# One scheduling priority in an RWKV scan: the merge of every pair's inverted blocks is ranked with the scan's steps

## The chip, the cores and the metric

The kernel runs on one core of a Trainium2 chip, as one launch. The metric is the device time of that launch in microseconds (us), less being better. Several executions are timed and their median is given; one further execution is recorded by the hardware profiler, and all rows shown here come from that one.

## The reference

The program computes two blocks of a network. The first block runs two layers of attention mixers (dilated attention with gated linear attention, then window attention with latent attention), each with a gated feed-forward part. The second block runs a gMLP mixer, a mixture of experts, an RWKV mixer and a second mixture of experts, on 512 tokens of grid data and 256 tokens of context, 1024 channels each. The change concerns the RWKV mixer alone, whose core is a recurrence over the tokens in both directions, for 16 heads of 64 channels:

```python
def _wkv_step(S, inp):
    r_t, w_t, k_t, v_t, a_t, b_t = inp
    sa = jnp.einsum('zbhvk,zbhk->zbhv', S, a_t)
    S = S * w_t[..., None, :] + sa[..., :, None] * b_t[..., None, :] + v_t[..., :, None] * k_t[..., None, :]
    return S, jnp.einsum('zbhvk,zbhk->zbhv', S, r_t)

def wkv_bidir(state0, scan_in):
    state, ys = lax.scan(_wkv_step, state0, scan_in)
    ys = jnp.moveaxis(ys, 0, 2)
    return state, ys[0] + ys[1][:, ::-1]
...
    state_c, y_c = wkv_bidir(state0, scan_c)
    _, y_l = wkv_bidir(state_c, scan_l)
```

The state of a head is a 64x64 matrix. It first goes through the 256 tokens of context, then through the 512 tokens of the grid.

## The kernel before

The class `_RwkvScan` does the recurrence in chunks of 64 tokens. The heads go in eight pairs, p0 to p7, and a pair has 12 scan steps (768 tokens in chunks of 64). One step works on both heads and both directions. Inside a chunk the recurrence is a triangular system, and its 64x64 triangle is inverted beforehand: two 32x32 diagonal blocks by substitution, and the block below them by two products, which is the merge that the change is about.

What a pair needs before its first step is made while the pair ahead of it is being scanned:

- **Elementwise preparation and triangles** (`pre`, L2309 to L2393): decays, keys and so on, on DVE and ACT; the triangles by PE matmuls L2376, masked by DVE L2381 into `AAx` (shown as tile `xT`). It runs two pairs ahead.
- **Substitution** (`load_tri`, `subst`, `back`): four DMAs L2404 take the triangles to DRAM, L2408 brings them back with another layout, GpSimd (POOL) substitutes column after column (L2420 and L2424, 31 times each), L2431 and four L2437 bring the result back through DRAM into `rwXT`, the tile of inverses, of which there are two.
- **Merge** (`merge`): DVE transposes the inverted blocks (L2449), PE multiplies (48 matmuls of 32x32 L2456), ACT evicts (four L2463), PE multiplies again (48 times L2471), and ACT evicts into `rwXT` (four L2479).
- **Operands** (`load_prep`, `prep`): DMA L2285 loads `inv`, PE makes products (L2516, L2522, 64 rows by 128), DVE masks them into `AAk` and `AAr` (L2525, L2527), PE transposes (L2531, L2540), ACT evicts (L2532, L2543), PE adds up within the chunk (L2555), ACT evicts (L2562, L2563). They come in three parts of four steps each; only the first must be there before the pair's first step.
- **Output** (`out`): DMA L2664 loads the gate into `AAk` (a name with two buffers, which the DVE masks use also), L2699 stores the result. From the seventh pair on the output projection (`project_out`) runs too: DMAs L2724, L2749 and L2751, matmuls in three float32 passes (L266 to L268), DVE L2739 and L245, ACT L244.

A scan step is a chain over the engines: DVE makes the right side `rwrz` (L2609, in a pair's first step L2611), PE multiplies it by the inverse `rwXT` (L2616), ACT evicts that as `UV` (L2620, one per step, called U below), PE updates the state (L2625), DVE adds it (L2634, L2636), and PE multiplies the new state for the next step (L2600, L2605).

`run` records the steps of a pair and between them the work of `beside`, in shares that fit the pair's length. The order of instructions on each engine is then decided by a scheduler, which ranks them by priority; inside `tc.high_priority(offset=400)` an instruction is ranked 400 ahead of where it was recorded. All scan steps are recorded so, and of the merges that of pair 7 alone. Every engine, and SP's queue of DMA issues, then runs its list in that order, and an instruction that waits holds all behind it.

Of the kernel before, what the change touches and what calls it, by code (L numbers as in the profile page):

```python
# [193 lines left out]
class Kern:  # L194
# [1718 lines left out]
    def rwkv_project(self, c, R, dr):  # L1913
# [76 lines left out]
        def full(j, w, name, ntok, ahead, beside, extra=None):  # L1990

            view = lambda f: [(0, w[:, f * P : (f + 1) * P])]
            early = [weights(view(f), P) for f in range(ahead)]
            cut = [(t0, min(T, ntok - t0)) for t0 in range(0, ntok, T)]
            outs = [[(self.pp.tile([P, 512], F32, tag="mm", name="mmps"), *c) for c in cut] for _ in early]
            x = []
            for d in range(KD):
                x.append(mix(j, d, ntok))
                for (H, L), out in zip(early, outs):
                    for ps, t0, n in out:  # L2000
                        self.mm3(
                            ps[:, :n], H[:, d, :], L[:, d, :], x[d][0][:, t0 : t0 + n], x[d][1][:, t0 : t0 + n],
                            d == 0, d == KD - 1,
                        )
            W = weights(view(ahead), P)
            for f in range(ahead):
                store(f, name, outs[f], ntok, extra)
            for f in range(ahead, KD):
                out = product(W, P, x, ntok)
                if f + 1 < KD:  # L2010
                    W = weights(view(f + 1), P)
                for _ in range(2 if f < KD - 1 else KD):
                    next(beside, None)
                store(f, name, out, ntok, extra)
# [49 lines left out]
        gate = []  # L2064
        beside = (s for g in (kk(), thin(5, [([(0, io["rw_g1"][:, a:b])], b - a) for a, b in ((0, 128), (128, 160))], T, gates)) for s in g)
        full(0, io["rw_wr"], "r", T, 2, beside)
        parts = []
        for n, sg, raw, wH, wL in gate:
# [38 lines left out]
class _RwkvScan:  # L2107
# [48 lines left out]
    def beside(self, p):  # L2156

        n = p + 1  # L2160
        inv = self.subst(n) if n < 8 else iter(())
        if n == 7:
            self.wo = self.project_out()
        wo = self.wo if n >= 7 else iter(())
        if n + 1 < 8:
            self.load_pre(n + 1)
        pre = self.pre(n + 1) if n + 1 < 8 else iter(())
        part = lambda g: iter(lambda: next(g, 0), 0)

        def operands():  # L2170
            if p >= 0:
                yield from part(self.gen)
                self.marks.add(("prep", p, 1))
            if p > 0:
                yield from self.out(p - 1)
                self.marks.add(("out", p - 1))
            if p >= 0:
                yield from self.gen
                self.marks.add(("prep", p, 2))
            if n < 8:  # L2180
                self.load_prep(n)
                self.gen = self.prep(n)
                yield from part(self.gen)
                while ("scan", p, 0) not in self.marks:
                    yield None
                yield from part(self.gen)
                self.marks.add(("prep", n, 0))

        def triangles():
            yield from pre  # L2190
            for _ in inv:
                if n == 7:
                    yield None
            if n < 8:
                self.back(n)
                self.marks.add(("subst", n))
            if n + 1 < 8:
                self.load_tri(n + 1)

        i, own, ahead = 0, operands(), triangles()  # L2200
        for w in own:
            yield w
            i += 1
            if i % 2 == 0:
                w = next(ahead, None)
                if w is not None:
                    yield w
            if n >= 7 and i % (2 if n == 7 else 1) == 0:
                w = next(wo, None)
                if w is not None:  # L2210
                    yield w
            for _ in range(2):
                next(inv, None)
        for w in ahead:
            if w is not None:
                yield w
        if n < 8:
            mg = self.merge(n)
            while True:
                with self.K.tc.high_priority(offset=400) if n == 7 else ExitStack():  # L2220
                    w = next(mg, None)
                if w is None:
                    break
                yield w
            self.marks.add(("merge", n))
        while ("scan", p, 2) not in self.marks:
            yield next(wo, None)
        if n == 8:
            yield from self.out(7)
            self.marks.add(("out", 7))  # L2230
            yield from wo
# [556 lines left out]
class _Sumsq:  # L2788
# [25 lines left out]
    def part(self):  # L2814
        if self.sums is None:
            self.flush()
            K, m = self.K, 32 * self.g
            self.sums = K.wk.tile([P, 512], F32, tag="sqs", name="sqs", bufs=1)
            K.nc.vector.tensor_copy(self.sums[:m, : self.n], self.ps[:m, : self.n])
        return self.sums[: 32 * self.g]  # L2820
# [110 lines left out]
```

## Time and profile before

| what | value |
|---|---|
| median of three timed executions | 4237.75 us (4226.5 to 4241.26) |
| profiled execution | 4238.35 us |
| its span, first to last instruction | 4236.2 us |
| mean granted TensorE clock over the span | 0.917 |
| the scan's steps, from the first U to the last | 3011.9 to 3621.3 us of the span |

How to read it: PE is TensorE, DVE is VectorE, ACT is ScalarE, POOL is GpSimd, SP issues the DMAs. A busy PE is not a PE at its peak: the granted clock is 1.00 at 2.4 GHz and 0.50 at 1.2 GHz, and a stretch between has part of each. The profiled execution has 2.15 us around its span. Times in the trace count from the start of the span.

### The profile page before, as it was taken

Reading aid. Unit: us, or ns where it says so; the run is one execution under the profiler, and the core shown is the slowest. Engines: PE = TensorE matmul, PEld = TensorE weight load, DVE = VectorE, ACT = ScalarE, POOL = GpSimd, SP = SyncE. Lnnn points to the kernel's source line nnn. Section 1 sums busy time; section 2 is a strip of 40 time slices with the busy share of each in tenths; the row PEclk is TensorE's granted clock in tenths of the full one; section 3 lists DMA queues with packets and bytes.
Section 4 is the critical chain, followed back from the end, with each engine's and each line's share of the span. In section 5 each row is a group of like instructions: output and inputs, shape, how many; then the busy total and the mean of one; then the engine's idle time right before and its main releaser. Section 6 shows DMA issues by size and latency. Waiting matters only on the chain. (4 is left out here: it accounts for less than half of the span.)

```text
span 4236.2 us, 56567 instructions
## 1 busy us (share of the span) xinstructions
PE 3829.5 (90%) x22652; PEld 2587.6 (61%) x22652; DVE 1814.1 (43%) x3656; ACT 1324.4 (31%) x2612; POOL 603.9 (14%) x829
## 2 busy tenths in 40 slices
PE   8989999999999989999788997997788899688886
PEld 6746777665677769887433333775577777433332
DVE  3443334465433534434422224554657655511112
ACT  3333224344322522234111112434446554200001
POOL 0000100000101000001110002001645442210001
PEclk9969999999999999999899998997768769799998
DMA  3212553211352322121699997342111222499997
GB/s 117 72 56 90 180 194 101 63 57 65 105 196 89 105 63 78 53 102 73 238 408 390 397 398 279 91 155 77 44 50 43 49 57 75 188 378 416 415 413 304
DMA packets 324825, 711.87 MB, mean 168 GB/s; under 512 B 79616, under 2 KB 251904, under 8 KB 299728
## 3 DMA queue, kind: packets, MB, share of 16 engines
q1 hardware_dynamic: 308704, 658.43, 42.7%
q0 software_dynamic: 15856, 49.79, 3.4%
q8 instruction: 180, 2.95, 0.3%
q14 instruction: 85, 0.70, 0.1%
HBM read 666.64 MB, written 47.55 MB: 169 GB/s over the span
## 5 line engine op out<-in xcount | busy, mean ns | idle before, releaser
L266 PE MATMUL mmps<-xH,wH 128*128 128x512 f32 (+1 forms) x1384 | 550.4, 399 | 10.7 <-ACT xH L359 8.2
L267 PE MATMUL mmps<-xL,wH 128*128 128x512 f32 (+1 forms) x1384 | 545.7, 394 | 0.0
L268 PE MATMUL mmps<-xH,wL 128*128 128x512 f32 (+1 forms) x1384 | 544.2, 394 | 0.0
L1488 PE MATMUL bgps<-wg,bxT 128*64 128x512 f32 (+2 forms) x1040 | 474.3, 601 | 0.9 <-issue 0.9
L1489 PE MATMUL bgps<-wu,bxT 128*64 128x512 f32 (+1 forms) x896 | 401.5, 602 | 26.3 <-DMA wu<-in_moe_w_up_dram 26.3
L244 ACT ACTIVATE wH<-wraw 128x512 fp32r<-128x512 f32 (+3 forms) x473 | 264.7, 619 | 500.4 <-PE mmps L267 289.8
L245 DVE TENSOR_TENSOR wL<-wraw,wH 128x512 fp32r<-128x512 f32 (+3 forms) x473 | 320.5, 723 | 212.2 <-ACT wH L244 211.7
L266 PEld LDWEIGHTS mmps<-xH,wH 128*128 128x128 f32 (+1 forms) x1384 | 258.8, 187 | 105.5 <-issue 22.1
L267 PEld LDWEIGHTS mmps<-xL,wH 128*128 128x128 f32 (+1 forms) x1384 | 258.8, 187 | 71.2 <-issue 10.8
L268 PEld LDWEIGHTS mmps<-xH,wL 128*128 128x128 f32 (+1 forms) x1384 | 258.5, 187 | 71.4 <-issue 11.8
L1505 PE MATMUL byps<-wd,bhT 128*64 128x512 f32 (+2 forms) x1040 | 292.5, 649 | 1.1 <-ACT bhT L1496 1.1
L1488 PEld LDWEIGHTS bgps<-wg,bxT 128*64 128x64 f32 (+2 forms) x1040 | 140.1, 138 | 213.8 <-issue 202.2
L1490 ACT ACTIVATE bh<-bgps 64x512 f32<-64x512 f32 (+2 forms) x65 | 38.4, 591 | 641.6 <-PE bgps L1489 545.1
L1489 PEld LDWEIGHTS bgps<-wu,bxT 128*64 128x64 f32 (+1 forms) x896 | 112.8, 129 | 121.9 <-issue 74.4
L1491 DVE TENSOR_TENSOR bh<-bgps,bh 64x512 f32<-64x512 f32 (+1 forms) x56 | 38.6, 690 | 341.1 <-ACT bh L1490 341.1
L2420 POOL TENSOR_TENSOR isub<-xT,rwX 96x31 f32<-96x31 f32 (+15 forms) x248 | 144.0, 581 | 262.9 <-DMA xT<-rwd 244.1
L1505 PEld LDWEIGHTS byps<-wd,bhT 128*64 128x64 f32 (+2 forms) x1040 | 86.5, 145 | 154.5 <-issue 148.8
L2424 POOL TENSOR_TENSOR rwX<-rwX,isub 96x31 f32<-96x31 f32 (+15 forms) x248 | 154.0, 621 | 19.4
L1454 POOL DMA_INDIRECT xg<-hnat,ix x65 | 62.7, 965 | 648.3 <-PE bxps L1476 609.6
L266 PE MATMUL mmps<-mH,pH 128*128 128x512 f32 (+2 forms) x336 | 123.5, 371 | 12.0 <-ACT pH L244 9.1
L532 POOL TENSOR_TENSOR ffng<-ffng,rstd 128x512 f32<-128x512 f32 x44 | 58.9, 1339 | 472.5 <-ACT ffng L531 472.5
L267 PE MATMUL mmps<-mL,pH 128*128 128x512 f32 (+1 forms) x336 | 124.2, 370 | 0.0
(741 smaller groups left out, 7441.4 us busy)
## 6 DMA issues: line engine op xcount, KB each, us to landing
wg<-in_moe_w_gate_dram SPq DMA_DIRECT2D x64, 2048.0 KB, 23.1
wu<-in_moe_w_up_dram SPq DMA_DIRECT2D x61, 2048.0 KB, 21.1
wd<-in_moe_w_down_dram SPq DMA_DIRECT2D x61, 2048.0 KB, 19.7
adaw<-in_ada_w_dram SPq DMA_DIRECT2D x48, 1024.0 KB, 5.0
wraw<-in_ffn_w_gate_dram SPq DMA_DIRECT2D x22, 1024.0 KB, 5.4
wraw<-in_ffn_w_up_dram SPq DMA_DIRECT2D x22, 1024.0 KB, 5.6
wraw<-in_ffn_w_down_dram SPq DMA_DIRECT2D x20, 1024.0 KB, 5.0
wraw<-in_ga_w_in_dram SPq DMA_DIRECT2D x16, 1024.0 KB, 5.6
```

Of the source, the lines that this page charges most:

```text
L244: self.nc.scalar.activation(H, src, AF.Copy)
L245: self.nc.vector.tensor_tensor(L, src, H.bitcast(F32), OP.subtract)
L266: nc.tensor.matmul(out, lh, rh, start=first, stop=False)
L267: nc.tensor.matmul(out, lh, rl, start=False, stop=False)
L268: nc.tensor.matmul(out, ll, rh, start=False, stop=last)
L532: nc.gpsimd.tensor_tensor(g[:, i, :], g[:, i, :], r, OP.mult)
L1454: self.gathered = self.nc.gpsimd.indirect_dma_start(out=x[:m, :], out_offset=None, in_=hnat, in_offset=bass.IndirectOffsetOnAxis(ap=it, ax ...
L1488: nc.tensor.matmul(og, xT[:, k, :m], wg[:, k, :], start=k == 0, stop=k == KD - 1, skip_group_check=True)
L1489: nc.tensor.matmul(ou, xT[:, k, :m], wu[:, k, :], start=k == 0, stop=k == KD - 1, skip_group_check=True)
L1505: nc.tensor.matmul(o[j], hT[:, k, :m], wd[:, k, j * 512 : (j + 1) * 512], start=k == 0, stop=k == 3, skip_group_check=True)
L2420: G.tensor_tensor(o, Lt[:96, :j, j : j + 1].to_broadcast((96, j, n)), X[:96, j : j + 1, j:].to_broadcast((96, j, n)), OP.mult,)
L2424: G.tensor_tensor(X[:96, :j, j:], X[:96, :j, j:], o, OP.add)
```

## The change

One line of `beside` (L2220): the condition falls, and the instructions of every pair's merge are recorded at high priority.

```diff
-                with self.K.tc.high_priority(offset=400) if n == 7 else ExitStack():
+                with self.K.tc.high_priority(offset=400):
                     w = next(mg, None)
```

No instruction comes or goes: as many as before stand on each engine, and GpSimd's list is the same. The order changes on PE, DVE, ACT and SP, from the first pair's merge to the end of the scan.

On SP's queue, at the triangles of pair 2 while pair 1 is scanned (rows with - stand there before, with + after the change; `rwd` is the copy in DRAM, `inv` the operand that L2285 loads):

```order
 L2404 DMA rwd_20703<-xT 32x24x32 x4
+L2664 DMA AAk<-rw_g 128x512
 L2285 DMA inv<-rw_v 128x768
 L2408 DMA xT<-rwd_20703 96x1024
-L2664 DMA AAk<-rw_g 128x512
 L2699 DMA rw_y<-AAk 128x512
```

The load of the gate, L2664, which stood behind the substitution's load L2408, stands ahead of it.

On the same queue, at the triangles of pair 7 while pair 6 is scanned:

```order
 L2724 DMA inr<-rw_y 128x512
+L2751 DMA rw_tw<-in_rw_wo_dram 128x5x128
 L2404 DMA rwd_25097<-xT 32x24x32 x4
 L2724 DMA inr<-rw_y 128x512
-L2749 DMA xT<-rw_x 128x512 x2
+L2664 DMA AAk<-rw_g 128x512
+L2285 DMA inv<-rw_v 128x768
 L2408 DMA xT<-rwd_25097 96x1024
-L2285 DMA inv<-rw_v 128x768
-L2749 DMA xT<-rw_x 128x512
-L2724 DMA inr<-rw_y 128x512
-L2664 DMA AAk<-rw_g 128x512
```

L2664 and L2285, which stood behind L2408, stand ahead of it; two L2749 went further up.

On PE, from the last step of pair 3 to the first of pair 4. Before (`x8` is eight matmuls in a row; the trace counts two for each of L2516, L2376 and L2456):

```order
L2616 MATMUL rwups<-rwrz_19417,rwXT_19410 64x64 x4
L2531 MATMUL rwtpps<-ident,BK 128x128
L2540 MATMUL rwtpps<-ident,inv 128x128 x2
L2540 MATMUL rwtpps<-ident,vrev 128x128
L2649 MATMUL rwryps<-UV,AAr 64x64 x4
L2540 MATMUL rwtpps<-ident,vrev 128x128
L2555 MATMUL rwtpps<-UV,AAk 64x64 x16
L2376 MATMUL rwaaps<-ARl,BK 64x64 x16
L2456 MATMUL rwtpps<-XoP,xT 32x32 x20
L2516 MATMUL rwaaps<-ARl,BK 128x128 x8
L2456 MATMUL rwtpps<-XoP,xT 32x32 x28
L2516 MATMUL rwaaps<-ARl,BK 128x128 x8
```

These are followed by 47 of the 48 L2471 and the L2616 of pair 4. After the change:

```order
L2616 MATMUL rwups<-rwrz_19417,rwXT_19410 64x64 x4
L2531 MATMUL rwtpps<-ident,BK 128x128 x6
L2649 MATMUL rwryps<-UV,AAr 64x64 x4
L2540 MATMUL rwtpps<-ident,inv 128x128 x2
L2540 MATMUL rwtpps<-ident,vrev 128x128 x2
L2555 MATMUL rwtpps<-UV,AAk 64x64 x16
L2456 MATMUL rwtpps<-XoP,xT 32x32 x48
L2376 MATMUL rwaaps<-ARl,BK 64x64 x4
L2471 MATMUL rwtpps<-rwXT_19409,XoP 32x32 x48
L2376 MATMUL rwaaps<-ARl,BK 64x64 x5
L2616 MATMUL rwups<-rwrz_19416,rwXT_19409 64x64 x4
```

The two blocks of eight L2516 inside the merge went behind the first L2616 of pair 4, and a part of L2376 too; the merge's own matmuls stand closer together.

## Rows read from the trace of the kernel before

**Rows 1.** Profile page: busy PE, and granted clock of 40 equal slices in tenths.
```profile
PE 3829.5 (90%) x22652; PEld 2587.6 (61%) x22652; DVE 1814.1 (43%) x3656; ACT 1324.4 (31%) x2612; POOL 603.9 (14%) x829
...
PEclk9969999999999999999899998997768769799998
```
**Rows 2.** U (L2620) by pairs, p5 left out: duration ns min/median/max, first and last start.
```profile
L2620 ACT ACTIVATE UV<-rwups x12: 377/378/379, 3011.9 to 3069.2; 64x256 f32<-64x256 f32 x12
...
L2620 ACT ACTIVATE UV<-rwups x12: 362/378/379, 3080.7 to 3148.2; 64x256 f32<-64x256 f32 x12
...
L2620 ACT ACTIVATE UV<-rwups x12: 377/378/380, 3166.1 to 3234.6; 64x256 f32<-64x256 f32 x12
...
L2620 ACT ACTIVATE UV<-rwups x12: 377/379/379, 3248.7 to 3302.2; 64x256 f32<-64x256 f32 x12
...
L2620 ACT ACTIVATE UV<-rwups x12: 377/379/380, 3320.6 to 3386.2; 64x256 f32<-64x256 f32 x12
...
L2620 ACT ACTIVATE UV<-rwups x12: 360/378/380, 3486.6 to 3542.4; 64x256 f32<-64x256 f32 x12
...
L2620 ACT ACTIVATE UV<-rwups x12: 377/379/381, 3566.7 to 3621.3; 64x256 f32<-64x256 f32 x12
```
**Rows 3.** Stretches: length, busy time and instructions by engine, granted clock, DMA share, GB/s.
```profile
3081.00:3111.00 30.00, 28.38 (x198) 21.11 (x198) 15.86 (x50) 16.35 (x38) 6.81 (x15) 0.61 0.13 36
...
3249.00:3268.00 19.00, 18.46 (x196) 14.26 (x195) 13.75 (x38) 13.57 (x31) 16.71 (x25) 1.00 0.13 37
3303.00:3321.00 18.00, 14.93 (x307) 13.60 (x308) 9.44 (x24) 7.29 (x17) 2.15 (x7) 0.67 0.45 105
3321.00:3352.00 31.00, 29.06 (x200) 21.66 (x201) 17.02 (x48) 14.07 (x32) 27.71 (x43) 0.61 0.08 22
...
3543.00:3567.00 24.00, 23.98 (x336) 19.27 (x335) 8.28 (x17) 11.36 (x21) 0.00 (x0) 1.00 0.32 97
```
**Rows 4.** Timeline, pair 3 to pair 4: start, duration, instruction, [idle before <-releaser].
```profile
3307.88 0.97 DVE L2449 STREAM_TRANSPOSE XoP<-rwXT 128x768 f32<-128x768 f32 x1
...
3309.00 1.15 PE L2456 MATMUL rwtpps<-XoP,xT 32*32 32x32 f32 x40 [0.96 <-DVE XoP L2449]
...
3310.08 2.08 PE L2516 MATMUL rwaaps<-ARl,BK 64*128 64x128 f32 x16
...
3313.73 3.09 PE L2516 MATMUL rwaaps<-ARl,BK 64*128 64x128 f32 x16
...
3316.75 2.76 PE L2471 MATMUL rwtpps<-rwXT,XoP 32*32 32x32 f32 x94
```
**Rows 5.** Timeline of ACT, pair 2 to pair 3.
```profile
3239.48 0.59 ACT L2563 ACTIVATE UV<-rwtpps 64x512 f32<-64x512 f32 x1
3243.63 1.98 ACT L2463 ACTIVATE XoP<-rwtpps 32x384 f32<-32x384 f32 x4 [3.55 <-PE rwtpps L2456]
3246.97 0.97 ACT L2479 ACTIVATE rwXT<-rwtpps 32x384 f32<-32x384 f32 x2 [1.37 <-PE rwtpps L2471]
```
**Rows 6.** Timeline of SP, then DVE, for pair 2's substitution.
```profile
3098.10 0.34 SPq L2285 DMA_DIRECT2D inv<-rw_v  x1
3098.62 0.32 SPq L2408 DMA_DIRECT2D xT<-rwd  x1
3102.88 0.34 SPq L2664 DMA_DIRECT2D AAk<-rw_g  x1
...
3153.31 0.98 DVE L2449 STREAM_TRANSPOSE XoP<-rwXT 128x768 f32<-128x768 f32 x1 [2.15 <-DMA rwXT<-rwd]
```
**Rows 7.** Timeline of SP, then DVE, for pair 7's substitution.
```profile
3481.40 0.33 SPq L2408 DMA_DIRECT2D xT<-rwd  x1
...
3504.80 0.32 SPq L2664 DMA_DIRECT2D AAk<-rw_g  x1
...
3529.45 2.04 SPq L2437 DMA_DIRECT2D rwXT<-rwd  x4
...
3542.14 0.96 DVE L2449 STREAM_TRANSPOSE XoP<-rwXT 128x768 f32<-128x768 f32 x1
```

## The prediction

> **What bounds the kernel now.** The page says that PE is busy for 90% of the span, and that the granted clock is low in one part, slices 28 to 33 of 40, where the scan lies [rows 1]. So I read the scan's stage alone, first by its one instruction per step, U [rows 2]. Eleven intervals lie inside a pair and one between pairs. Inside pair 3 they average (3302.2 - 3248.7)/11 = 4.9 us, inside pair 1 6.1 us. Between pairs, from the last U to the next first, they are 11.5 (0 to 1), 17.9, 14.1, 18.4 (3 to 4) and 24.3 us (6 to 7); 4 to 5 and 5 to 6, together with pair 5 itself, fill the 100.4 us from 3386.2 to 3486.6, and I cost both as 3 to 4. So the pauses between the pairs are what a merge that is ranked higher can shorten.
>
> Then I read the stretches. The four first steps of pair 3, at a clock of 1.00, take 19 us; those of pair 4, with as much PE work (200 matmuls for 196), take 31 us at 0.61 [rows 3]. Pair 1 starts at 0.61 too, and pairs 2, 5 and 6 low in the same way; 3 and 7 don't. **A pair that starts at half clock thus costs some 11 us more**, a larger sum than any pause that the change can shorten.
>
> Third, the pause itself, 3 to 4 [rows 4]: DVE comes to the transpose L2449 at 3307.88, behind the triangles' elementwise chain, PE waits for it (0.96 us idle ahead of L2456), does the merge with two blocks of L2516 inside it (2.08 and 3.09 us), and then L2471. Nothing there is waiting for the substitution. Only between pairs 1 and 2 the transpose waits for it (2.15 us for the DMA) [rows 6].
>
> **The change part by part.** No instruction is added. The sum goes against the profiled execution, 4238.35 us, 0.6 us above the median.
>
> *The pauses.* At 0 to 1 the transpose goes up by two steps, and the merge's matmuls go among the last three steps; after the last U there remain 24 L2471, two pairs of L2479 and the L2616: a quarter of 2.76 x 2 us, 2 x 0.97, about 1, so 3.5 instead of 11.5: -8 us. What goes among the steps isn't free: a transpose of 0.97 and the merge's matmuls between links of the chain, +1.5. In pair 0 the last eviction goes ahead of the first U as well, +1. At 2 to 3 the transpose and L2516 leave the pause, but ACT's queue doesn't get shorter: it ends L2563 at 3240.1, 5.4 us after the last U, and then has four L2463 (1.98) and four L2479 (2 x 0.97) with PE between [rows 5]. That adds up to about 10 instead of 14.1: -4. At 3 to 4 the same limit gives about 11 instead of 18.4: -7.4, and as much at 4 to 5 and 5 to 6: together -22.
>
> *What goes out of the pause comes back.* The two blocks of L2516 are wanted by the pair's later steps, so they run in its first four steps, where PE is busy for 18.46 of 19 or 29.06 of 31 us [rows 3]; nothing hides them. They are 5.2 us in the pause [rows 4], at half clock for the second of them at least; I take 4 for each of three pairs, and 3 for pair 3, whose pause is at full clock: +15. The bounds are 0 (all in idle ends of the steps) and 5.2 each.
>
> *SP's queue at pair 2.* L2664 waits for a buffer of `AAk`, which pair 1's own steps set free; the load L2408 stood ahead of it and will stand behind it and L2285, at 3102.88 + two issues of 0.52, some 5.3 us later [rows 6]. From there to the arrival of the inverses POOL and the DMAs need 54.7 us (3098.6 to 3153.3), and DVE already waits for them, so that all of it counts. Two things stand against it: pair 1's first steps come sooner if it starts at full clock, and behind the transpose there is less than before (12.8 us to the next U, 8.3 without L2516). If the clock holds at 0 to 1, where PE has merge work in each of the last three steps, it is -4 for this pair; if it doesn't, about +4. I take -4, with 0.7.
>
> *The clock at 2 to 3.* This pause holds the full clock now, with PE busy on L2516 in it (pair 3 starts at 1.00, [rows 3]). With L2516 gone the pause is shorter, but what is left of it has PE waiting on ACT. I take it that pair 3 then starts as the five others do: +11, the difference of the two rows. No row shows such a pause; the bounds are 0 and 12.
>
> *SP's queue at pair 7.* L2408 stands behind L2664 and L2285: 3504.80 for 3481.40, 24 us later with the issues. The inverses landed by about 3533 (the L2437 begin at 3529.45, with some 3.6 us to their end), and were used at 3542.14 [rows 7]: 9 us of slack, so up to 15 us come through. Beside them stand the passes of the output projection, which fill PE in the pause before (23.98 of 24 us, [rows 3]), and they can be done while it waits. DVE's transpose, though, holds the evictions behind it, and with them PSUM's buffers, so that PE can't go on with all of them. I take +8, between 0 and 15, nearer to the middle since half of PE's work of the pause is the projection's.
>
> *The sum*: +1 - 8 + 1.5 - 4 - 22 + 15 - 4 + 11 + 8 = -1.5 us. That is 4236.9 against the profile, and 4236 on the median's side.
>
> On the clock the rows show this: five pauses of 11.5 to 18.4 us are followed by a low clock, and one of 14.1 isn't; it isn't length alone that decides. The Trainium skill, page "TensorE: Matmul & The Clock Gate", section "HAM oscillation — how this bites in real kernels", says that a kernel whose matmul bursts are parted by waits has each burst begin at the low clock, and that it stays high where the work between covers the wait. By that the shorter pauses should rather hold the clock, which is the first rival; the trace agrees only in part, since the pause from 6 to 7, the longest, but filled by PE to 23.98 of 24 us, starts pair 7 high [rows 3].
>
> **Rivals.** (1) *The shorter pauses hold the clock.* Condition: PE's idle stretches in the pause, now the wait for L2449 and for ACT's evictions, shrink with it. Each pause held gives 11 us, and the loss at 2 to 3 doesn't come. For it: the merge is off the pause at 0 to 1 altogether. Against it: at 3 to 4 the pause loses more PE work (5.2 of L2516) than idle time. With 2 to 3 and two others held: 4236 - 11 - 22 = 4203. With 2 to 3 alone: 4225.
>
> (2) *The substitution becomes the bound at pairs 2 and 7*, slower than before: a DMA that was issued first now waits in SP's queue behind one that needs a buffer of the running scan. Its place is L2408; its price is +8 at pair 2 against the forecast (clock not held at 0 to 1), and +7 more at pair 7, if PE runs out of work: 4236 + 15 = 4251. It decides from the point at which L2408 is later than the 9 us of slack. For it: the order is certain, and 2.15 us of waiting are there today. Against it: pair 1 may run faster, and the projection can fill.
>
> (3) *The pauses don't get shorter*, because ACT's chain and not the transpose sets them: then the -26 from 2 to 6 is gone, the clock at 2 to 3 stays (no +11), and half of the +15 for L2516 is done in idle time: 4236 + 26 - 11 - 8 = 4243.
>
> **How the numbers follow.** About 0.3% (12.7 us, so 4225.0 and 4250.5) can be told from no change. The forecast with its neighbours inside these bounds has 0.36, rival 3 has 0.08, together 0.44; rival 1 has 0.31, of which some 0.1 below 4205; rival 2 has 0.25, of which 0.09 above 4257. The range that leaves out no more than 2 in 10 is 4205 to 4257; the bounds of single terms (L2516 0 to 15.6, the clock 0 to 12, pair 7 0 to 15) lie inside. Faster 0.31, same 0.44, slower 0.25.
>
> **What will show it.** In the new trace the first and last U of each pair give the pauses: 3.5 at 0 to 1, 10 at 2 to 3, 11 at the next three. The stretches over each pair's first steps give the clock: pair 1 high, pair 3 low, 4 to 6 low. SP's rows show L2408 of pair 2 behind L2664, and of pair 7 some 24 us later against its pair's first U; the idle time ahead of L2449 at pair 7 says DMA. The forecast is wrong if pairs 3 to 6 start at full clock (faster), or if the interval from pair 6's first U to pair 7's, 80.1 us now [rows 2], grows by 12 or more (slower).

## The result: slower by 0.9%, and the profile after

| | before | after |
|---|---|---|
| median of seven executions | 4237.75 us (4226.34 to 4252.69) | 4277.32 us (4258.59 to 4283.34) |
| profiled execution | 4238.35 us | 4258.59 us |
| mean granted clock over its span | 0.917 | 0.915 |
| scan, first U of pair 0 to last U of pair 7 | 609.4 us | 630.6 us |

The ratio is 1.0093, with an interval of 1.0069 to 1.0117: slower by some 40 us, outside the range of the prediction. The profiled execution of after is the shortest of its seven, so its trace shows only half of the loss: 20.2 us against the profile of before. The scan, from pair 0's first U to pair 7's last, is 21.2 us longer in it. A second profile of the same kernel (e1_again, 4301.69 us, below) shows more than the whole of it; the two are read together.

The page of after, busy engines and granted clock of 40 slices, for [rows 1]:

```profile
PE 3850.1 (90%) x22652; PEld 2596.3 (61%) x22652; DVE 1821.5 (43%) x3656; ACT 1325.9 (31%) x2612; POOL 599.9 (14%) x829
...
PEclk9969999999999999999899998996688769799998
```

The number of instructions is the same on each engine; PE is busy 20.6 us longer. The low slices are again those of the scan.

U by pairs, after, for [rows 2] (duration ns min/median/max, first and last start):

```profile
L2620 ACT ACTIVATE UV<-rwups x12: 377/378/380, 3014.4 to 3072.9; 64x256 f32<-64x256 f32 x12
L2620 ACT ACTIVATE UV<-rwups x12: 370/378/378, 3076.9 to 3135.4; 64x256 f32<-64x256 f32 x12
L2620 ACT ACTIVATE UV<-rwups x12: 377/378/379, 3162.3 to 3234.0; 64x256 f32<-64x256 f32 x12
L2620 ACT ACTIVATE UV<-rwups x12: 359/378/379, 3244.8 to 3307.4; 64x256 f32<-64x256 f32 x12
L2620 ACT ACTIVATE UV<-rwups x12: 361/378/378, 3319.7 to 3390.8; 64x256 f32<-64x256 f32 x12
L2620 ACT ACTIVATE UV<-rwups x12: 365/378/378, 3407.4 to 3480.3; 64x256 f32<-64x256 f32 x12
L2620 ACT ACTIVATE UV<-rwups x12: 365/378/380, 3491.7 to 3564.4; 64x256 f32<-64x256 f32 x12
L2620 ACT ACTIVATE UV<-rwups x12: 377/378/381, 3590.3 to 3645.0; 64x256 f32<-64x256 f32 x12
```

From the last U of a pair to the first of the next: 4.0 us, 26.9, 10.8, 12.3, 16.6, 11.4 and 25.9. Five of the seven pauses did shrink (before: 11.5, 17.9, 14.1, 18.4, 18.5, 18.7 and 24.3). The pairs themselves grew: pair 4 takes 71.1 us from its first to its last U for 65.6, pair 6 72.7 for 55.8.

The stretches of after, for [rows 3]: the first four steps of pairs 3, 4, 5 and 6, and the pause from 3 to 4 (length, then busy us and instructions of PE, PEld, DVE, ACT and POOL, granted clock, DMA share, GB/s):

```profile
3244.80:3269.70 24.90, 22.73 (x226) 17.49 (x226) 19.95 (x45) 13.10 (x29) 14.93 (x26) 0.98 0.24 60
3319.70:3357.20 37.50, 37.50 (x240) 29.08 (x242) 20.47 (x49) 13.46 (x30) 25.55 (x42) 0.54 0.16 39
3407.40:3444.60 37.20, 37.20 (x221) 28.71 (x221) 18.84 (x40) 12.74 (x28) 27.33 (x45) 0.50 0.15 38
3491.70:3526.50 34.80, 34.80 (x205) 27.89 (x206) 12.01 (x31) 9.63 (x22) 3.24 (x9) 0.52 0.27 69
3307.40:3319.70 12.30, 9.85 (x267) 8.82 (x270) 6.64 (x16) 9.06 (x20) 0.00 (x0) 0.74 0.31 89
```

What left the pause stands in the steps behind it. Pair 3, at full clock in both kernels, takes 24.9 us for its first four steps, for 19.7 before (cut at the same steps); pair 4, whose first three steps are at half clock in both, 37.5 for 30.9; pair 6 34.8 for 23.3, with more work and less clock. In three of the four the profile shows PE busy throughout. Pair 6's four steps before:

```profile
3486.60:3509.90 23.30, 23.30 (x179) 18.30 (x179) 8.31 (x27) 10.75 (x24) 20.40 (x38) 0.63 0.27 80
```

The moved work can be seen by itself. These are stretches with the matmuls into `rwaaps` (L2516 and L2376) alone, pause 3 to 4 and then the first four steps of pair 4. Before:

```profile
3302.20:3320.60 18.40, 6.19 (x64) 5.46 (x64) 4.40 (x12) 0.69 0.46 109
3320.60:3351.50 30.90, 8.37 (x46) 6.17 (x46) 2.91 (x8) 0.61 0.08 23
```

After:

```profile
3307.40:3319.70 12.30, 1.49 (x22) 1.11 (x26) 0.76 (x2) 0.74 0.31 89
3319.70:3357.20 37.50, 17.82 (x88) 13.49 (x88) 6.84 (x18) 0.54 0.16 39
```

4.70 us of PE's time left the pause and 9.45 came up in the steps, 42 matmuls in both cases: most of them now run at half clock.

### The profile page after: what moved, and what is told of

Read it like the earlier page. It is cut to its first block, busy times and chain, and to the rows that moved or that the text cites. A ratio compares the mean times of both kernels' runs of the same rounds, so it can differ in the third digit from the quotient of the medians.

```text
span 4256.8 us, 56570 instructions
## 1 busy us (share of the span) xinstructions
PE 3850.1 (90%) x22652; PEld 2596.3 (61%) x22652; DVE 1821.5 (43%) x3656; ACT 1325.9 (31%) x2612; POOL 599.9 (14%) x829
## 5 line engine op out<-in xcount | busy, mean ns | idle before, releaser
L267 PEld LDWEIGHTS mmps<-xL,wH 128*128 128x128 f32 (+1 forms) x1384 | 258.8, 187 | 71.3 <-issue 10.8
L2420 POOL TENSOR_TENSOR isub<-xT,rwX 96x31 f32<-96x31 f32 (+15 forms) x248 | 142.6, 575 | 298.9 <-DMA xT<-rwd 280.0
```

Source lines behind the costliest of these rows:

```text
L267: nc.tensor.matmul(out, lh, rl, start=False, stop=False)
L2420: G.tensor_tensor(o, Lt[:96, :j, j : j + 1].to_broadcast((96, j, n)), X[:96, j : j + 1, j:].to_broadcast((96, j, n)), OP.mult,)
```

## The experiments

All ratios are against the kernel before, run beside it on the same chip. A pair is said to **start low** when its first three steps take 19 us or more (the others take 12 to 18, the longer ones with a part at half clock). That is counted at the four pauses from 2 to 3 up to 5 to 6, which are alike in the work they hold.

### e1_again and e5_base: both kernels unchanged, a second time

> The changed kernel once more, unaltered, for a second profile of it: its first profiled execution (4258.6 us) was the shortest of its seven timed ones (median 4277). Crowding theory (what the pauses between the pairs lose comes back as work of PE in each pair's first four steps, at half clock): the same intervals from first U to first U as in the first profile, within 3 us each: 62, 85, 82, 75, 88, 84, 99; time 0.5 to 1.1% over before. If the clock alone makes the spread between executions, one or two of the intervals will be longer by some 10 us, with a lower clock in those pairs' first steps, and all the others equal.

> The kernel before, unaltered, for a second profile. In two profiles of the changed kernel the same order of instructions gave intervals from first U to first U of 85.4 and 94.9 (pair 1), 82.5 and 90.9, 74.9 and 81.6, 84.3 and 91.7 us (pair 5) at a granted clock of 0.80 and 0.68, 0.79 and 0.67, 0.87 and 0.77, 0.74 and 0.63. If the clock varies in the kernel before as well, some of its intervals will differ from the first profile's (69, 85, 83, 72, 84, 82, 80) by 5 to 10 us, at another clock; if it is a trait of the changed order, all agree within 2 us.

Measured: e1_again 4285.58 us, 1.0111 (1.0078 to 1.0143); e5_base, a single execution, 4234.16 us. Intervals from first U to first U, us, with the granted clock (the last row goes on to pair 7's last U):

| pair | before | e5_base | after | e1_again | mean after - mean before |
|---|---|---|---|---|---|
| 0 | 68.8 at .82 | 68.5 at .77 | 62.5 at .83 | 60.5 at .89 | -7.1 |
| 1 | 85.4 at .70 | 88.9 at .71 | 85.4 at .80 | 94.9 at .68 | +3.0 |
| 2 | 82.6 at .73 | 80.4 at .74 | 82.5 at .79 | 90.9 at .67 | +5.2 |
| 3 | 71.9 at .90 | 75.8 at .79 | 74.9 at .87 | 81.6 at .77 | +4.4 |
| 4 | 84.0 at .70 | 77.1 at .79 | 87.7 at .71 | 86.2 at .74 | +6.4 |
| 5 | 82.0 at .73 | 79.5 at .76 | 84.3 at .74 | 91.7 at .63 | +7.3 |
| 6 | 80.1 at .89 | 73.3 at 1.00 | 98.6 at .80 | 98.4 at .80 | +21.8 |
| scan | 609.4 at .80 | 598.1 at .81 | 630.6 at .81 | 658.8 at .75 | +41.0 |

The mean difference of the scans, 41.0 us, is near the difference of the medians, 39.6. With two profiles of each kernel, so near an agreement is in part luck: the two scans of the changed kernel alone differ by 28.2 us, and their profiled executions by 43.1, so that some 15 us of the scatter lie outside the scan. The loss lies in every pair but the first, and half of it in pair 6.

The expectation was missed in one point: four intervals of the changed kernel moved by 7 to 10 us, where one or two were expected.

What was new is the spread within one kernel. Pair 4 in the profile of the kernel before (a stretch, as above):

```profile
3320.60:3404.60 84.00, 76.88 (x855) 61.23 (x856) 50.14 (x133) 46.52 (x103) 37.62 (x64) 0.70 0.18 45
```

and in e5_base:

```profile
3333.70:3410.80 77.10, 69.62 (x856) 56.41 (x855) 50.54 (x133) 46.22 (x104) 40.60 (x66) 0.79 0.19 49
```

Pair 1 in the profile of after:

```profile
3076.90:3162.30 85.40, 67.89 (x864) 53.90 (x864) 53.24 (x127) 46.89 (x103) 39.74 (x64) 0.80 0.20 53
```

and in e1_again:

```profile
3086.00:3180.90 94.90, 78.98 (x864) 62.05 (x864) 51.51 (x127) 46.60 (x104) 41.11 (x64) 0.68 0.19 47
```

The same instructions in the same order take 7 to 10 us more or less, and it is the clock that differs between these rows, not the work. In e5_base the pause 5 to 6 is 14.1 us and pair 6 starts at full clock; in the profile of before it was 18.7 and low. So the state "five of six pauses lose the clock", on which the prediction stood, was one draw of several.

### e2_not6: all merges ranked ahead but that of pair 6

```diff
-                with self.K.tc.high_priority(offset=400):
+                with self.K.tc.high_priority(offset=400) if n != 6 else ExitStack():
```

> The change without the merge of pair 6 (ranked as before there, all others ahead). SP's queue then keeps the old order at pair 7: L2408 ahead of L2285 and L2664. Queue theory (L2408 behind them is what costs at pair 7) and crowding theory (pair 6's first steps have the postponed products and the output projection's passes at half clock) both say that pair 6's first U to pair 7's goes from 99 back to 80 to 83 us, with the interval before it 3 to 5 longer than before; total 14 to 18 us below the changed kernel, +0.3 to +0.6% over before. If pair 6's interval stays above 92, the cause lies in an earlier pair's merge and both fall.

Measured: 4250.92 us, 1.0045 (1.0028 to 1.0063). Pair 6 of e2_not6:

```profile
3494.80:3569.80 75.00, 73.02 (x822) 56.76 (x821) 39.47 (x100) 40.57 (x88) 35.62 (x62) 1.00 0.33 93
```

It takes nearly what it takes in e5_base, in the order of before and at full clock too:

```profile
3490.30:3563.60 73.30, 72.42 (x822) 56.90 (x821) 40.26 (x100) 40.56 (x88) 35.41 (x62) 1.00 0.33 96
```

What follows: without the merge of pair 6 about half of the loss is gone, as the table of pairs said (1.0093 and 1.0111 against 1.0045).

### e7_only6: the merge of pair 6 alone ranked ahead

```diff
-                with self.K.tc.high_priority(offset=400):
+                with self.K.tc.high_priority(offset=400) if n in (6,7) else ExitStack():
```

> The change for the merge of pair 6 alone. In the order pair 6's first four steps hold 28 of the 32 products (16 before), and at pair 7 L2285 stands ahead of the load L2408, with L2664 behind it as before. Crowding and queue theories together: pair 6's first U to pair 7's grows from 80 to 92 or more, the interval ahead of it shrinks by 3 to 7, all other pairs as before; total +5 to +15 us. If only L2664 matters in the queue and crowding is nothing: 78 to 84 us, total within 6 us of before.

Measured: 4249.87 us, 1.005 (1.0025 to 1.0076). Pair 6, nearly at full clock here:

```profile
3482.90:3567.30 84.40, 78.00 (x840) 60.97 (x837) 42.13 (x109) 40.48 (x86) 35.19 (x62) 0.96 0.31 87
```

Of the 11 us to e5_base (73.3 at 1.00), 7.1 lie in the pause from pair 6 to 7, 31.4 us for 24.3. There DVE and ACT wait:

```profile
3545.22 0.98 DVE L2449 STREAM_TRANSPOSE XoP<-rwXT 128x768 f32<-128x768 f32 x1 [5.88 <-DMA rwXT<-rwd]
...
3547.35 0.74 ACT L244 ACTIVATE ink<-rw_tw 128x640 fp32r<-128x640 f32 x1 [8.29 <-DMA rw_tw<-in_rw_wo_dram]
```

The transpose waits for the inverses, since L2408 is issued 10.0 us after the pair's first U (5.2 ahead of it in the profile of before), behind L2285. ACT waits for a load of weights, L2751, which SP issues behind the substitution's L2437.

What follows: from the other side, a loss of the same size, though SP's order at pair 7 is not the change's own (L2664 stands behind L2408 here). With pair 6 near full clock, the substitution is the bound at pair 7, as the prediction feared. After and e1_again, which start pair 6 low, take 14 us more, and there the transpose hardly waits.

### e3_poolload: the change, with the substitution's load issued by GpSimd

```diff
-        self.last = nc.sync.dma_start(self.Lt[:96], d1)
+        self.last = nc.gpsimd.dma_start(self.Lt[:96], d1)
```

> The changed kernel with one difference: the load L2408 of the triangles is issued from GpSimd's queue and not from SP's, so that nothing of SP's queue stands ahead of it. Queue theory: L2408 of pair 7 is issued some 20 us sooner, and pair 6's interval goes from 99 to 85 or less; total 10 to 18 us below the changed kernel. Crowding theory: the substitution starts sooner, but pair 6's first four steps stay at 33 to 36 us with PE full, and its interval stays at 92 or more; total within 6 us of the changed kernel.

Measured: 4262.1 us, 1.0063 (1.0037 to 1.009). The pause 1 to 2 falls from 26.9 us (24.8 in e1_again) to 16.3, and pair 6 from 98.6 to 82.7:

```profile
3496.10:3578.80 82.70, 81.31 (x854) 63.73 (x854) 43.96 (x110) 40.72 (x87) 35.82 (x63) 0.96 0.31 84
```

What follows: SP's queue had a part in both places, as rival 2 of the prediction said, and taking it away leaves more than half of the loss. In this profile pair 6 also starts better (three steps of 15.8 us at 0.79, for 26.9 at 0.50), so not all of the 16 us need be the queue's; these runs don't part the two.

### e16_pool: the kernel before, with the same load on GpSimd

```diff
-        self.last = nc.sync.dma_start(self.Lt[:96], d1)
+        self.last = nc.gpsimd.dma_start(self.Lt[:96], d1)
```

> The kernel before, with only the load L2408 issued from GpSimd's queue. SP's order there has L2408 ahead of L2664 and behind L2285 at pair 2 only, so the queue can cost little: pair 1's interval 84 to 86 us for 85 to 89, all others as before within the clock's scatter; time within 0.3% of before. If the queue matters more than thought: 0.3% or more faster.

Measured: 4237.24 us, 1.0016 (0.9978 to 1.0054). Its profile has a short pause 1 to 2 (15.3 us), and the interval holds no change. In the order of before the queue is no bound worth mending.

### e4_only4: the merge of pair 4 alone ranked ahead

```diff
-                with self.K.tc.high_priority(offset=400):
+                with self.K.tc.high_priority(offset=400) if n in (4, 7) else ExitStack():
```

> The change for the merge of pair 4 alone (pair 7's as before), all others as before. SP's order stays as it was but for L2699 ahead of the L2437. Crowding theory: the pause from pair 3 to 4 goes from 18 to 11 or 12 us, pair 4's first four steps grow by 6 to 10, so that first U of pair 3 to first U of pair 5 (155.9 before) changes by -2 to +4; total within 0.15% of before. Pause theory (the pause is pure loss): -6 to -7 us, 0.15% faster.

Measured: 4259.65 us, 1.0062 (1.0036 to 1.0089). In its profile pair 3 loses the clock in its late steps (85.9 us at 0.69), the pause 3 to 4 is 17.6 us and not 12, and pair 4 starts low (24.7 us for three steps; 88.1 us at 0.73 in all). A single merge costs 0.6%, where no more than 0.15% either way was expected, and more than the change without pair 6's merge (1.0045): the shares of the merges don't add up. Neither the pause that it should shorten nor the moved products (some 5 us) explain that without the clock.

### e8_only1p: the merge of pair 1 alone, load on GpSimd

```diff
-                with self.K.tc.high_priority(offset=400):
+                with self.K.tc.high_priority(offset=400) if n in (1,7) else ExitStack():
...
-        self.last = nc.sync.dma_start(self.Lt[:96], d1)
+        self.last = nc.gpsimd.dma_start(self.Lt[:96], d1)
```

> The change for the merge of pair 1 alone, and the load L2408 issued from GpSimd's queue, so that SP's order has no part in it. Pair 1's merge then lies among pair 0's last steps, and no pair's first steps get more products. All theories: pair 0's interval 61 to 63 for 69, the rest as before, 4 to 8 us less in all (0.1 to 0.2% faster), if the clock at pair 1's start doesn't fall; if clock luck is what decides, the total can lie 10 us to either side.

Measured: 4223.67 us, 0.9984 (0.9958 to 1.0011). Pair 0 is 63.6 us for 68.5 to 68.8, with a pause of 6.7 us, and pair 1 starts low (24.0 us). Ahead of pair 1 the merge gains some 5 us in pair 0, as expected; in the time of the whole that can't be told from no change.

### e6_off50 and e12_off25p: a smaller rank

```diff
-                with self.K.tc.high_priority(offset=400):
+                with self.K.tc.high_priority(offset=(50 if n < 7 else 400)) if True else ExitStack():
```

e12_off25p has 25 in the place of 50, and L2408 on GpSimd as above.

> The change with the merges of pairs 0 to 6 ranked 50 ahead and not 400. In the order the merge's matmuls then stand ahead of the next pair's products, but these stay in the pause: 12 to 16 of the 32 L2516 there and 16 to 20 in the first four steps, as before the change (16 and 16), for 0 to 4 and 28 to 32 with the change. SP's order is as before but for pair 2. Crowding theory: the loss of pairs 3 to 6 goes, pair 0 to 1 keeps its 6 us: within 0.3% of before (-8 to +6 us). Clock theory (the early transposes and the interleaved merges make the clock fall more often, the products have no part in it): still 0.4% or more over before.

> The change with the merges of pairs 0 to 6 ranked only 25 ahead, and the load L2408 on GpSimd's queue. Pauses from 2 to 5 hold 12 to 21 products, and the first block stands right behind L2376 and ahead of the merge (before: inside its first half; ranked 50 ahead: behind the whole first half, with all four pauses falling). Clock theory: 1 or 2 of 4 pauses fall, time within 8 us of before, or below. If an early merge by itself makes the clock fall: 3 or 4 of 4, and 0.4% or more over before, as with 50.

Measured: 4264.72 us, 1.0079 (1.0049 to 1.011), and 4246.21 us, 1.0035 (1.0009 to 1.0062). With 50, 12 to 16 of the 32 products (L2516 as the order lists them) of each pair still stand in the pause, where before has 16 and the change none to four; yet all four pairs start low, and the scan takes 646.3 us. With 25 two of four start low. What follows: the moved products can't be the whole of it; the order with 50, in between, loses the clock as often as the change.

### e9_prod1, e14_prod1_again: the other way, more products in the pause

Not the merge but the operands' products are taken forward: one share of the generator `self.gen` (which `prep` feeds) ahead of each merge of pairs 1 to 6, in the kernel before.

```diff
         if n < 8:
+            for _ in range(1 if 0 < n < 7 else 0):
+                yield next(self.gen)
             mg = self.merge(n)
```

> The kernel before (merges ranked as before), with the first block of eight L2516 of each pair's second operand part recorded ahead of the merge: 24 of the 32 products then lie in the pause (before 16, changed kernel 0 to 4) and 8 in the first four steps (16; 28 to 32). So far, at the pauses from 2 to 3 up to 5 to 6, the clock fell for the whole start of the next pair (its first three steps 19 us or more) in 7 of 19 with the order of before, in 14 of 17 with the change's. Theory that products in the pause hold the clock: at most 1 of 4 falls here, and the time is 5 to 25 us below before. Theory that they are only moved work: pauses longer by 1 to 2 us, first steps shorter by as much, clock falling as often as before (1 or 2 of 4), time within 6 us of before.

> The kernel with 24 products in the pause, unaltered, for a second profile. If its order holds the clock: again at most 1 of the 4 pauses from 2 to 6 falls, the intervals of pairs 2 to 6 are 70 to 80 us. If the first profile was luck: 2 or more fall, with intervals of 80 us or more.

Measured: 4204.11 us over 12 executions, 0.9928 (0.9903 to 0.9952): **faster than both kernels**, by 0.7% than the one before. The second execution, e14_prod1_again, took 4196.37 us. 24 of a pair's 32 products stand in the pause now, and 8 in its first four steps. The pause 3 to 4, the first four steps of pair 4, and pair 4's interval:

```profile
3297.80:3311.90 14.10, 13.03 (x324) 11.47 (x324) 9.49 (x25) 7.08 (x16) 0.31 (x2) 1.00 0.52 133
3311.90:3332.80 20.90, 18.41 (x186) 13.83 (x186) 15.38 (x39) 13.29 (x32) 18.55 (x31) 0.94 0.11 33
...
3311.90:3383.60 71.70, 64.79 (x856) 51.02 (x856) 52.97 (x133) 45.58 (x104) 38.40 (x63) 0.88 0.21 53
```

Pair 4's interval in e14_prod1_again:

```profile
3310.30:3382.10 71.80, 64.63 (x856) 50.85 (x855) 52.96 (x133) 45.58 (x103) 38.08 (x63) 0.88 0.21 53
```

The clock holds through the pause, and the two executions agree within 0.1 us in this pair (within 2 us in pairs 2 to 6), where the kernel before has 84.0 and 77.1. The pause on PE (start, duration, instruction, [idle before <-releaser]; L2518 is L2516 of before, by two added lines):

```profile
3300.61 1.03 PE L2557 MATMUL rwtpps<-UV,AAk 128*64 128x64 f32 x28
...
3301.58 0.95 PE L2458 MATMUL rwtpps<-XoP,xT 32*32 32x32 f32 x48
...
3303.94 1.17 PE L2518 MATMUL rwaaps<-ARl,BK 64*128 64x128 f32 x16
...
3306.04 1.79 PE L2518 MATMUL rwaaps<-ARl,BK 64*128 64x128 f32 x16 [0.24 <-DVE AAr L2529]
...
3308.10 1.79 PE L2518 MATMUL rwaaps<-ARl,BK 64*128 64x128 f32 x16
```

Products lie where PE would wait for the transpose and the evictions; at full clock a block of 16 takes 1.17 to 1.79 us, for 2.08 and 3.09 in [rows 4]. Its longest wait in the pause is 0.4 us, before 1.5.

### e15_prod1_pool, e13_change_prod1: the two together with others

e15 is e9_prod1 with L2408 on GpSimd; e13 is the change with the two added lines of e9_prod1.

> The kernel with 24 products in the pause, and the load L2408 issued from GpSimd's queue. If SP's queue still costs something at pairs 2 and 7: 2 to 8 us below the run with 24 products alone (ratio to before 0.990 to 0.993). If not: the same ratio, 0.993 within 0.003.

> The change (every merge ranked 400 ahead) with the first product block recorded ahead of the merge, as in the run with 24 products in the pause. In the order the merge then goes ahead of the products all the same: 0 to 7 of 32 in the pause, 25 to 32 in the first four steps, and PE waits for ACT ahead of L2555 as in the changed kernel. Theory that the place decides (work of PE in the waits of the pause): 3 or 4 of the 4 pauses from 2 to 6 fall, the time is 0.6 to 1.3% over before. Theory that the recording by itself does it (all that follows is earlier): 20 us or more below the changed kernel, so at most +0.6%.

Measured: e15 4208.52 us, 0.9975 (0.9936 to 1.0014), with a profile at 4193.89; e13 4269.27 us, 1.0077 (1.004 to 1.0115). In e13 the merge still goes past the products: none to 7 of 32 are in the pause, three of four pairs start low, and its scan takes 643.6 us. The gain of e9_prod1 needs the merge's rank of before. The median of e15 is near that of e9_prod1, but fewer executions stood beside it and the kernel before scattered widely among them, so that a gain isn't shown by it. In e15 all four pairs start high again, although three of its pauses have a wait of 1.5 us on PE: the longest wait alone doesn't decide.

### e10_prod3, e11_prod3_1p: three shares ahead

```diff
+            for _ in range(3 if 0 < n < 7 else 0):
+                yield next(self.gen)
             mg = self.merge(n)
```

e11_prod3_1p has this with the merge of pair 1 ranked ahead and L2408 on GpSimd.

> As the run with 24 products in the pause, but three blocks are recorded ahead of the merge (both blocks of L2516 and the first transposes): 30 of 32 products in the pause, none in the first four steps. Theory that products in the pause hold the clock: 0 or 1 of 4 falls, time 10 to 30 us below before. Theory that they are only moved work: pauses longer by 3 to 5 us, the first steps shorter by that, 1 or 2 of 4 falls, time within 8 us of before. If long pauses are what makes the clock fall, more falls (3 or 4 of 4) and a time over before.

> The run with 30 products in the pause, and with it the merge of pair 1 alone ranked 400 ahead and the load L2408 on GpSimd's queue (which together gave a ratio of 0.9984 to before, 0.9958 to 1.0011). If the parts add up: 5 to 8 us below the run with 30 products alone. If pair 1's start loses the clock with it, as in all profiles so far where pair 1's merge was ranked ahead (5 of 5), as much as that run.

Measured: 4253.29 us, 1.0047 (1.0018 to 1.0076), and 4239.23 us, 1.0023 (0.9995 to 1.0051). None of the expectations for e10 fits whole: one of the four pauses falls, as the first said, and yet the time is above that of before. 30 of 32 products stand in the pause, which is 13.1 us where the clock holds; but pair 3 of e10 starts low, and then loses the clock once more inside the pair. The pause ahead of pair 3, pair 3 whole, its first 15 us, and the next 38:

```profile
3239.70:3257.70 18.00, 17.54 (x300) 15.90 (x300) 7.87 (x20) 3.59 (x8) 0.00 (x0) 0.67 0.19 40
3257.70:3339.80 82.10, 77.45 (x857) 61.46 (x856) 51.51 (x133) 45.84 (x104) 40.26 (x64) 0.76 0.18 46
3257.70:3273.00 15.30, 15.30 (x105) 10.81 (x104) 4.81 (x11) 7.18 (x17) 5.32 (x12) 0.50 0.22 65
3273.00:3311.00 38.00, 34.33 (x267) 27.15 (x267) 24.64 (x69) 21.56 (x47) 33.67 (x51) 0.68 0.03 10
```

Pair 3 takes 82.1 us, for 72.1 in e9_prod1. In the pause ahead of it PE is busy for 17.54 of 18.00 us and the clock falls all the same: a fall doesn't need a long wait of PE (the longest is 0.46 us here). In e11 pairs 3 and 4 start low. So more products in the pause are not better without end, and shorter pauses of 13.1 us are not worth what the clock takes in the steps. Why the clock goes with 30 where it holds with 24 is not settled by these runs.

## Why the prediction was wrong, point by point

The step that failed is the clock: +11 for pair 3, and nothing for pairs 4 to 6, whose low starts were taken as given. The order of the change starts 14 of 17 pairs low, that of before 8 of 23 (counted below). Beside it three sizes were off: the four pauses save 15 and not 26 us, the products cost 5 to 11 us a pair and not 3 to 4, and pair 6 loses 21.8 us. Added up by interval from pair 0 to pair 6, the terms on record are -5.5, -4, -4, +6.6, -3.4, -3.4 and +12. The mean differences in the table above lie 7 to 11 us higher for pairs 1, 2, 4, 5 and 6. Pair 3 came near its +6.6 by luck: it starts low in one of its two profiles and not in the other.

**Right: the pauses' own lengths.** Forecast 3.5 at 0 to 1, 10 at 2 to 3, 11 at the next three; measured 4.0, 10.8, 12.3, 16.6 and 11.4 (e1_again 4.0, 12.7, 12.4, 16.4, 11.9). Pair 0's interval, +1 - 8 + 1.5 on record, is -6.3 in the profile and -7.1 in the mean. So the lengths that were worked out from ACT's queue came near for three of four, and missed 4 to 5, at 16.6; that this queue alone sets them isn't shown.

**Wrong by half: what those pauses save.** -26 was taken for the four, from 14.1 and three of 18.4. The second profile of the kernel before has 14.1, 18.5, 18.5 and 14.1. In the order of before 14.1 is the length where the clock holds, and 18.4 mostly that where it falls inside. The means of two profiles each give -2.4, -6.1, -2.0 and -4.8, so -15.3.

**Wrong in size: the products that come back**, +15, at 3 to 4 us a pair with 5.2 as the bound (for four pairs that bound is 20.8; the 15.6 beside the range counts three). For pair 3, at full clock in both profiles, the first four steps are 5.2 us longer; for pair 4, with three steps at half clock in both, 6.6; for pair 6, where all four steps are at half clock after, 11.5. The bound was the time that two blocks take in the pause. But the trace counts 64 L2516 in the first four steps (two for each product) for 32 before, and DVE gets work behind them. After, DVE around the fourth step of pair 4:

```profile
3345.10 0.60 DVE L2636 SCALAR_TENSOR_TENSOR S<-rwsps,P,SP 128x128 f32<-128x128 f32 x2
...
3352.56 1.65 DVE L2353 SCALAR_TENSOR_TENSOR ARc<-inq,sg 128x256 f32<-128x256 f32 x2
3354.24 0.43 DVE L2609 TENSOR_TENSOR rwrz<-rwryps,UV 64x256 f32<-64x256 f32 x1
```

Between the state L2636 and the next right side L2609 stand 8.5 us of the next pairs' preparation. The fourth step alone takes 12.8 to 15.5 us in pairs 2 to 5 after, 6.7 to 9.8 before. This link of the chain was not in the sum.

**Wrong in kind: the clock.** +11 was set for 2 to 3 and nothing for the others, as if a low start elsewhere could not get more frequent because it was there already. In the profile of after 2 to 3 even holds (12.1 us for three steps); it is lost in e1_again, e2_not6 and e3_poolload (21.3 to 21.4). Over all profiles with one of three orders at the pause (e6, e10 to e13 have others):

| order at the pause | 2 to 3 | 3 to 4 | 4 to 5 | 5 to 6 | low in all |
|---|---|---|---|---|---|
| of before | 2 of 6 | 1 of 5 | 4 of 6 | 1 of 6 | 8 of 23 |
| of the change | 3 of 4 | 5 of 5 | 4 of 4 | 2 of 4 | 14 of 17 |
| one share of products ahead (e9, e14, e15) | 0 of 3 | 0 of 3 | 0 of 3 | 0 of 3 | 0 of 12 |

At the two pauses ahead of these, 0 to 1 and 1 to 2, the products don't protect: with one share ahead, pair 1 starts low in all three profiles, pair 2 in two, and pair 2's pause too holds 24 products. The counts come from few profiles of kernels that differ elsewhere.

The profile on which the prediction rested was the one of five with a fall at 3 to 4, and the one of six at 5 to 6. The change's own frequency is 1.9 low starts more per execution (3/4 - 2/6, 1 - 1/5, 1 - 4/6, 2/4 - 1/6, added). At 7 us each, by 84.0 against 77.1 of pair 4 and 80.1 against 73.3 of pair 6, they come to an estimate of 13 us, where the sum on record has +11 for 2 to 3 alone. Rival 1 stood the other way round: the change's shorter pauses lose the clock more often, not less.

What PE waits for in them can be seen. After, PE in the pause 3 to 4, for [rows 4]:

```profile
3311.83 0.95 PE L2456 MATMUL rwtpps<-XoP,xT 32*32 32x32 f32 x48
...
3313.21 1.45 PE L2456 MATMUL rwtpps<-XoP,xT 32*32 32x32 f32 x48 [0.43 <-ACT UV L2563]
...
3339.95 2.07 PE L2516 MATMUL rwaaps<-ARl,BK 64*128 64x128 f32 x8
```

The products are gone from between the merge's small matmuls, and come at 3339.95, where eight take what sixteen took before. PE is idle for 2.5 us of the 12.3, for 3.1 of 18.4 before and 1.1 of 14.1 in e9_prod1. The prediction cited the Trainium skill, page "TensorE: Matmul & The Clock Gate", section "HAM oscillation — how this bites in real kernels", for bursts that start low behind waits. The trace agrees where products cover the waits at the four pauses (0 of 12), but not with the reading that a shorter pause is safer: 14 of 17 pauses of 10.8 to 17.6 us lost it, and e10_prod3 lost it in one that PE filled to 17.54 of 18.00 us.

**Right in kind, twice mis-sized: SP's queue.** Pair 2, after, for [rows 6]:

```profile
3095.81 0.34 SPq L2664 DMA_DIRECT2D AAk<-rw_g  x1
3096.80 0.33 SPq L2408 DMA_DIRECT2D xT<-rwd  x1
...
3151.26 0.98 DVE L2449 STREAM_TRANSPOSE XoP<-rwXT 128x768 f32<-128x768 f32 x1 [7.54 <-DMA rwXT<-rwd]
```

L2408 stands behind L2664, and the transpose waits 7.54 us for the inverses, for 2.15. The sum took -4 here, with the clock held at 0 to 1. It wasn't held in full: pair 1's first three steps take 17.6 us in the profile, and 25.1 in e1_again. The +4 of the other branch is near the +3.0 of the mean. Pair 7, after, for [rows 7], with the eighth step of pair 6:

```profile
3516.39 0.34 SPq L2664 DMA_DIRECT2D AAk<-rw_g  x1
3517.38 0.33 SPq L2408 DMA_DIRECT2D xT<-rwd  x1
...
3541.34 0.32 SPq L2749 DMA_DIRECT2D xT<-rw_x  x1
3541.75 0.38 SPq L2724 DMA_DIRECT2D inr<-rw_y  x1
...
3545.05 0.63 ACT L244 ACTIVATE ARl<-inr 128x512 fp32r<-128x512 f32 x1 [3.27 <-DMA inr<-rw_y]
3545.73 0.80 PE L266 MATMUL rwaaps<-ARl,ink 128*128 128x512 f32 x1 [2.87 <-ACT ARl L244]
...
3572.50 0.98 DVE L2449 STREAM_TRANSPOSE XoP<-rwXT 128x768 f32<-128x768 f32 x1 [1.09 <-DMA rwXT<-rwd]
```

Against its pair's first U, L2408 is 31 us later (+25.7 for -5.2); 24 were forecast. But little came by the way foreseen: the transpose waits 1.09 us, and the pause 6 to 7 grew by 1.6. The slack of 9 us grew with the pair: each step that is slower gives the substitution time. Another load was met instead. L2749 needs a buffer that the late substitution still reads (SP waits 9.8 us for POOL's L2420), and L2724 stands behind it. ACT waits 3.27 us for L2724 ahead of the projection, PE 2.87 for ACT, and the step takes 11.2 us for 5.5. Pair 6 in the profile is thus +18.5 = 11.5 (first four steps) + 5.7 (eighth step) + 1.6 (pause), to within 0.3. Where pair 6 runs near full clock, in e7_only6, the wait that was foreseen does come: 5.88 us, and a pause 7.1 us longer for the +8 on record. The prediction's own mark for "slower", pair 6's interval growing by 12 or more, is what came, though mostly by another way than the queue.

**In all.** Of the mean +41.0, the order alone, at nearly equal clock, is an estimate of +14: pair 0 -7, pairs 3 to 5 some +3 each (84.0 at 0.70 against 87.7 at 0.71; 82.0 at 0.73 against 84.3 at 0.74; 71.9 at 0.90 against 74.9 at 0.87), and pair 6 +11 (73.3 at 1.00 against 84.4 at 0.96, a part of it clock) give +13, and the waits of pair 1 about +1 to +3. By another count it is +21: the scans of the first profile of either kernel, at 0.80 and 0.81, have the same share of low clock and differ by 21.2 us. In these two it isn't more low clock that costs, but more of the work standing where the clock is low. The remaining +20 to +27 go with the clock: 13 for the additional low starts, the rest argued and not counted apart, in pairs that start low in both but stay so for longer, and in falls in late steps (e4_only4). What makes the chip lower the clock in one execution and not in the next of the same kernel stays open, and so does the share of either cause to better than these 7 us.

## What to carry to other kernels

Before an instruction is ranked out of a pause, see what independent work it will push into the chain behind, and on every in-order queue what it leaves waiting: here the gain was in the opposite edit, more of the independent products in the pause (0.9928). Before a sum rests on which stretches run at the low clock, take a second profile of the unchanged kernel; two of them differ by 11 us in this scan.

## What the runs showed of the hardware

That the granted clock stays at half for a long time with PE busy throughout was not expected: 37.20 of 37.20 us busy at a granted clock of 0.50 (pair 5 after), 34.80 of 34.80 at 0.52 (pair 6). In the profiles of after and e1_again the clock comes back 42 to 47 us behind the last U of the pair ahead, where pairs 4 and 6 start low; ahead of and in pair 5 of e1_again it stays at 0.50 for 68.3 us (3427.8 to 3496.1), with PE busy for 66.80 of them. Nor was it expected that the clock falls with PE busy for 17.54 of 18.00 us (e10_prod3). Nor was it expected that a single-core program gives such different clocks in its pairs from one execution to the next, 85.4 us at 0.80 and 94.9 at 0.68 in pair 1 of one kernel, while another order of the same instructions (e9_prod1 and e14_prod1_again) repeats pair 4's interval within 0.1 us (e9_prod1's pair 5 differs by 1.9).
